# A Mamba-2 layer inside a trunk kernel: TensorE's steps placed by hand, diagonal parts by pairs

## The chip, the cores and the metric

The kernel runs on one core of one Trainium2 chip. A core has TensorE (PE, matrix products into PSUM), VectorE (DVE), ScalarE (ACT, activations from tables), GpSimd (POOL) and SyncE (SP, which here issues all DMAs). Each engine works through its own instructions in order and waits at semaphores for the others. The metric is the device time of one execution in microseconds (us); lower is better.

## The reference

Two layers of a decoder trunk on 512 tokens of 1024 features. Each has a token mixer, a squared-ReLU MLP, two layer norms and a gated embedding. The change touches only the mixer of the first layer, Mamba-2 SSD: 32 heads of 64 columns in 4 groups, 4 chunks of 128 tokens. Cut to that mixer:

```python
zxbcdt = u @ w_in
z, xbc, dt = jnp.split(zxbcdt, [SSD_D_INNER, SSD_D_INNER + SSD_CONV_DIM], axis=-1)
xbc = jax.nn.silu(causal_depthwise_conv(xbc, conv_w, conv_b))       # 4 taps
xs, bm, cm = jnp.split(xbc, [SSD_D_INNER, SSD_D_INNER + SSD_BC_DIM], axis=-1)
dt = jax.nn.softplus(dt + dt_bias)
da = dt * -jnp.exp(a_log)
xdt = xs * dt[..., None]
a_cs = jnp.cumsum(da, axis=2)                                        # within a chunk
decay = segsum_exp(jnp.moveaxis(da, 2, -1))
cb = jnp.einsum('bclgn,bcsgn->bcgls', cm, bm)
y_diag = jnp.einsum('bcgls,bcgrls,bcsgrp->bclgrp', cb, decay, xdt)
decay_to_end = jnp.exp(a_cs[:, :, -1:] - a_cs)
states = jnp.einsum('bclgn,bclgr,bclgrp->bcgrpn', bm, decay_to_end, xdt)
chunk_decay = jnp.exp(a_cs[:, :, -1])
# scan over the chunks: h <- h * chunk_decay + states; prev is the h that a chunk starts with
y_off = jnp.einsum('bclgn,bcgrpn,bclgr->bclgrp', cm, prev, jnp.exp(a_cs))
y = y_diag + y_off + d_skip * xs
y = y * jax.nn.silu(z)
y = rms_norm(y by groups, norm_w)
return y @ w_out
```

## The kernel before

[...] I call these three matmuls of 512 columns a triple. A weight unit is 128 x 1024 numbers. `unit` (line 102) loads one by DMA into one of three `raw` buffers and `split` (line 109) makes its two parts: a cast on ScalarE (`whi`, line 113, six buffers) and a subtraction on VectorE (`wlo`, line 115, six buffers). Both are given a high priority, so that they are issued well ahead of the product.

The SSD mixer works by tiles j = 0 to 15 of 128 inner features, that is two heads each; a group is four tiles. Features lie on partitions, the 512 tokens in the free dimension. For a tile:

- `xz` (line 675) projects x and z with eight triples each. The first goes through `conv_silu` (line 628): a scaled copy on ScalarE, three taps on VectorE (line 634), silu on ScalarE (line 635). The second goes through silu alone (line 683). Before a group's first tile, `bc_group` (line 647) does the same for the group's B and C, and `bc_prep` (line 656) turns B to tokens on partitions (`btok`) and makes the masked products of C and B (`cbm`).
- `core` (line 686) loads the tile's cumulated decays from DRAM (`csb`), turns xs to tokens (line 693), multiplies it by dt (`xdt`, line 701) and by the decay to the chunk's end (`xw`, line 700). Three products with `btok` give the chunks' states (line 705); the chain from chunk to chunk is a copy, and for each of two further chunks a product and a sum (lines 712 to 715). The decay matrix `m` takes eight subtractions, an exponential and a product with `cbm` (lines 721 to 725). Eight matmuls on 64 columns each give the diagonal part (`yd`, line 735), three more the part carried from the states (`yo`, line 741). Lines 748 to 751 put y together.
- The group's output product `ssd_out` (line 775) runs once the group's root mean square is there: `rms_group` (line 762) sums the squares on TensorE (line 767, on 64 columns again) and takes the square root on ScalarE (line 771).

The loop over j (from line 783) writes these parts one after the other: projections of tile j, then `core` of tile j - 1. The order on each engine is not the written one: a planner with priorities places all instructions, those of TensorE too, by what it expects of their times. PSUM has eight banks: four for projections (`pj`), one for transposes and sums (`pt`), one for states (`pm`), two for `py0` (diagonal) and `py1` (carried). Of the work buffers, xs, z and the convolution have two each, `xdt`, `xw`, `pv`, `ecs` and `y` one. ScalarE holds one table of functions at a time; going from silu to exp or to the square root means a table load (ACT_TABLE_LOAD).

Of the kernel before, what the change touches and what calls it, by code (L numbers as in the profile page):

```python
# [15 lines left out]
P = 128  # L16
# [28 lines left out]
def trunk(ctx: ExitStack, tc, a):  # L45
# [25 lines left out]
    def f32(t):  # L71
        return t.bitcast(F32)

    two = dict(xs=2, sz=2, cv=2, cm=2, cbm=2)
    mlp = dict(r=8, blk=2, sg=2)
    bufs = dict(ssd=dict(two, ss=2), mlp0=mlp, hgrn=dict(two, xs=4, sz=4, cv=4, y=2, pv=2, btok=2, sc=2, scb=2, qd=2), mlp1=mlp)
    phase = []

    def begin(name):
# [539 lines left out]
    def dt_tail():  # L619
# [5 lines left out]
        nc.vector.tensor_copy(t, pt[:, : 3 * P].rearrange("p (i c h) -> p i c h", i=3, c=NCH))  # L625
        return t[:, 0], t[:, 2], t[:, 1]

    def conv_silu(ps, i, out):

        cv = tmp("cv", [P, T])  # L630
        nc.scalar.activation(cv, ps, AF.Identity, scale=convw[:, i, 3:4], bias=convb[:, i : i + 1])  # L631
        for k in range(3):
            d = 3 - k
            nc.vector.scalar_tensor_tensor(cv[:, d:], ps[:, : T - d], convw[:, i, k : k + 1], cv[:, d:], ALU.mult, ALU.add)  # L634
        nc.scalar.activation(out, cv, AF.Silu)
# [3 lines left out]
    def projected(i):  # L639

        if i < 4:
            return first[i]
        ps = bank(psj, "pj")
        project(unit(wssd[i - 4]), x_s, ps)
        return ps

    def bc_group(g):
        bcm = []
        for which in range(2):
            ps = projected(10 * g + which)  # L650
            t = tmp(("bm", "cm")[which], [P, T])
            conv_silu(ps, 16 + 4 * which + g, t)
            bcm.append(t)
        return bcm

    def bc_prep(bcm):
# [5 lines left out]
        nc.scalar.copy(btok, pt[:, : 3 * P].rearrange("p (c n) -> p c n", c=3))  # L662
# [8 lines left out]
        return btok, cbm, cm  # L671

    toks = []

    def xz(j):
        ps = projected(10 * (j // 4) + 2 + 2 * (j % 4))
        xs = tmp("xs", [P, T])
        conv_silu(ps, j, xs)
        if j == 1:
            toks.extend(dt_tail())  # L680
        ps = projected(10 * (j // 4) + 3 + 2 * (j % 4))
        sz = tmp("sz", [P, T])
        nc.scalar.activation(sz, ps, AF.Silu)
        return xs, sz

    def core(j, xs, sz, y, toks, btok, cbm, cm, ss=None):
        dt_tok, w_tok, cs_tok = toks
        csb = mk(w4, [P, 2, T], "a")
        nc.sync.dma_start(csb, bass.AP(tensor=csd.tensor, offset=csd.offset + 2 * j * T, ap=[[0, P], [T, 2], [1, T]]))

        pt = bank(pst, "pt")
        for c in range(NCH):
            nc.tensor.transpose(pt[:, c * P : (c + 1) * P], xs[:, c * P : (c + 1) * P], ident)  # L693
        xdt = tmp("xdt", [P, 8, 64])
        v = pt.rearrange("p (c h q) -> p (c h) q", c=NCH, h=2)
        xdt4 = xdt.rearrange("p (c h) q -> p c h q", c=NCH)
        hs = slice(2 * j, 2 * j + 2)
        ptv = pt.rearrange("p (c h q) -> p c h q", c=NCH, h=2)
        xw = tmp("xw", [P, 3, 2, 64])
        nc.vector.tensor_mul(xw, ptv[:, 0:3], bc(w_tok[:, 0:3, hs], 3, 64))  # L700
        nc.vector.tensor_mul(xdt4, ptv, bc(dt_tok[:, :, hs], 3, 64))

        pst_ = bank(psm, "pm")
        for c in range(3):
            nc.tensor.matmul(  # L705
                pst_[:, c * P : (c + 1) * P], btok[:, c, :], xw[:, c].rearrange("p h q -> p (h q)"), start=True, stop=True
            )
        cd = mk(sm, [P, 2, NCH], "cd")
        nc.scalar.activation(cd, csb.rearrange("p h (c l) -> p h c l", c=NCH)[:, :, :, P - 1], AF.Exp)
        pv = tmp("pv", [P, 3, 2, 64])  # L710
        stv = pst_[:, : 3 * P].rearrange("p (c h q) -> p c h q", c=3, h=2)
        nc.vector.tensor_copy(pv[:, 0], stv[:, 0])
        for c in range(1, 3):
            nc.vector.tensor_mul(pv[:, c], pv[:, c - 1], bc(cd[:, :, c], 2, 64))
            nc.vector.tensor_add(pv[:, c], stv[:, c], pv[:, c])

        m = mk(w4, [P, 2, T], "b")
        for r in range(2):
            for c in range(NCH):
                sl = slice(c * P, (c + 1) * P)  # L720
                nc.vector.tensor_scalar(
                    m[:, r, sl], csb[:, r, sl], cs_tok[:, c, 2 * j + r : 2 * j + r + 1], 0.0, ALU.subtract, ALU.min
                )
        nc.scalar.activation(m, m, AF.Exp)
        nc.vector.tensor_mul(m, m, bc(cbm, 1, 2))

        ecs = tmp("ecs", [P, 3 * P])
        for r in range(2):
            rs = slice(64 * r, 64 * r + 64)
            nc.scalar.activation(ecs[rs], csb[rs, r, P:], AF.Exp)  # L730
        yd = bank(psy, "py0")
        for c in range(NCH):
            sl = slice(c * P, (c + 1) * P)
            for r in range(2):
                nc.tensor.matmul(  # L735
                    yd[64 * r : 64 * r + 64, sl], xdt[:, 2 * c + r, :], m[:, r, sl], start=True, stop=True
                )
        ri = None if ss is None else rms_group(ss)
        yo = bank(psy, "py1")
        for c in range(1, NCH):  # L740
            nc.tensor.matmul(  # L741
                yo[:, c * P : (c + 1) * P],
                pv[:, c - 1].rearrange("p h q -> p (h q)"),
                cm[:, c * P : (c + 1) * P],
                start=True,
                stop=True,
            )
        nc.vector.scalar_tensor_tensor(y, xs, dskip[:, j : j + 1], yd, ALU.mult, ALU.add)
        nc.vector.tensor_mul(ecs, yo[:, P:], ecs)
        nc.vector.tensor_add(y[:, P:], y[:, P:], ecs)  # L750
        nc.vector.tensor_mul(y, y, sz)
        return ri

    def sq_sum(y, ss):
        sq = tmp("ss" if ss is None else "sq", [P, T])
# [16 lines left out]
        nc.vector.reciprocal(ri, ri)  # L772
        return ri

    def ssd_out(g, s, ri, *after):
        out_project(a["wso"][4 * g : 4 * g + 4], s, False, *after, scale=ri)

    pend = None
    ys = None
    bcm = None  # L780
    prep = None
    outs = []
    for j in range(17):
        nbcm = bc_group(j // 4) if j % 4 == 0 and j < 16 else None
        cur = xz(j) if j < 16 else None
        if j == 4:
            nc.sync.dma_start(acc, a["x"])
            for c in range(NCH):
                nc.vector.tensor_scalar(acc[:, c, :], acc[:, c, :], ALPHA, None, ALU.mult)
        if pend is not None:  # L790
            i = j - 1
            if i % 4 == 0:
                ys = Split(4)
                ss = None
                prep = bc_prep(bcm)
            y = tmp("y", [P, T])
            due = bool(outs) and (i % 4 == 1 or i == 15) and i != 13
            ri = core(i, *pend, y, toks, *prep, outs[0][2] if due else None)
            w = snw[:, i : i + 1]
            nc.scalar.activation(ys.h(i % 4), y, AF.Copy, scale=w)  # L800
            nc.vector.scalar_tensor_tensor(ys.l(i % 4), y, w, f32(ys.h(i % 4)), ALU.mult, ALU.subtract)
            ss = sq_sum(y, ss)
            if i % 4 == 3:
                outs.append((i // 4, ys, ss))
            if due:
                ssd_out(*outs.pop(0)[:2], ri)
        if nbcm is not None:
            bcm = nbcm
        pend = cur
# [460 lines left out]
```

## Time and profile before

| | us |
|---|---|
| median of three runs | 1425.13 |
| lowest, highest | 1424.92, 1426.70 |
| the profiled execution, device time | 1426.6 |
| its span, first to last instruction | 1424.8 |
| PE busy in the span | 1413.6 (99%) |
| DVE busy | 1057.4 (74%) |
| ACT busy | 754.5 (53%) |

The page lists how long each engine is busy; in the views by time, a row has start, duration, engine, line, operation, and which tile is written from which. In brackets stands how long the engine was idle before it and who released it. The granted clock of TensorE is 1.00 throughout. In the views by groups, `x32 | 9.1, 284 | 0.1` means 32 instructions, 9.1 us busy, 284 ns each on the mean, and 0.1 us of idle time just before them. A float32 matmul of 128 columns stands in the profile as two instructions, a transpose as one.

### The profile page before, as it was taken

The numbers are of one execution on the slowest core, as the hardware profiler recorded it, in microseconds if no ns is written. First come the engines' busy times: TensorE is split into PE (matmuls) and PEld (weight loads), VectorE is DVE, ScalarE is ACT, GpSimd is POOL, SyncE is SP. The second block draws the span as 40 slices with busy tenths as digits, with TensorE's granted clock in tenths as the row PEclk, the third lists the DMA queues.
The fourth block names the chain that finished last, engine by engine and source line by source line (L and its number), as shares of the span: only waits on it lengthen the run. The fifth ranks groups of instructions, "written<-read, shape, count | busy, mean of one in ns | idle before, by whom it ended". The sixth has DMA issues, their size and how long they took to land.

```text
span 1424.8 us, 20421 instructions
## 1 busy us (share of the span) xinstructions
PE 1413.6 (99%) x8061; PEld 1174.6 (82%) x8061; DVE 1057.4 (74%) x1760; ACT 754.5 (53%) x1134; POOL 1.8 (0%) x12
## 2 busy tenths in 40 slices
PE   9999999999999999999999999999999999999998
PEld 7888888888888888888888887887898888888887
DVE  7988687787967667677986576678685867667873
ACT  6776454563265454545545547655555454544641
POOL 0000000000000000000000000000000000000000
PEclk9999999999999999999999999999999999999999
DMA  8432323333433444444621321222163444444231
GB/s 298 142 130 92 119 89 119 104 107 126 152 119 121 158 130 153 133 148 163 215 82 49 133 90 60 75 90 90 50 232 104 148 137 145 148 133 163 89 118 45
DMA packets 49392, 178.02 MB, mean 125 GB/s; under 512 B 5521, under 2 KB 6289, under 8 KB 49169
## 3 DMA queue, kind: packets, MB, share of 16 engines
q1 hardware_dynamic: 49296, 176.73, 36.8%
q8 instruction: 63, 1.03, 0.3%
q14 instruction: 33, 0.26, 0.1%
HBM read 174.54 MB, written 2.16 MB: 124 GB/s over the span
## 4 chain that ended last, share of the span: by engine, by line
PE 94%; DVE 3%; ACT 2%; DMA 1%; issue 0%; SPq 0%; ACTq 0%; DVEq 0%
PE pj L119 23%; PE pj L120 23%; PE pj L121 23%; PE py L119 5%; PE py L121 5%; PE py L120 5%; PE py L735 1%; PE py L741 1%; PE py L981 1%; PE pm L705 1%; DVE wlo L115 1%; PE pt L233 1%; PE pt L693 1%; DMA r<-in_w 1%; PE py L1107 0%
## 5 line engine op out<-in xcount | busy, mean ns | idle before, releaser
L113 ACT CAST whi<-raw 128x1024 fp32r<-128x1024 f32 x222 | 233.0, 1052 | 330.3 <-PE pj L120 234.1
L119 PE MATMUL pj<-b,whi 128*128 128x512 f32 (+1 forms) x1006 | 382.1, 381 | 0.7 <-ACT b L237 0.7
L120 PE MATMUL pj<-b,whi 128*128 128x512 f32 (+1 forms) x1006 | 380.6, 379 | 1.0 <-DVE b L238 1.0
L121 PE MATMUL pj<-b,wlo 128*128 128x512 f32 (+1 forms) x1006 | 379.2, 377 | 0.0
L115 DVE TENSOR_TENSOR wlo<-raw,whi 128x1024 fp32r<-128x1024 f32 x222 | 269.8, 1220 | 142.2 <-ACT whi L113 136.8
L120 PEld LDWEIGHTS pj<-b,whi 128*128 128x128 f32 x1006 | 189.4, 188 | 34.2 <-DVE b L238 1.2
L119 PEld LDWEIGHTS pj<-b,whi 128*128 128x128 f32 x1006 | 188.9, 188 | 34.1 <-ACT b L237 0.9
L121 PEld LDWEIGHTS pj<-b,wlo 128*128 128x128 f32 x1006 | 189.2, 188 | 33.6
L121 PE MATMUL pj<-whi,b 128*128 128x512 f32 x544 | 212.8, 392 | 0.0
L119 PE MATMUL pj<-whi,b 128*128 128x512 f32 x536 | 212.7, 397 | 0.0
L120 PE MATMUL pj<-wlo,b 128*128 128x512 f32 x536 | 210.2, 393 | 0.0
L121 PEld LDWEIGHTS pj<-whi,b 128*128 128x128 f32 x544 | 102.1, 188 | 20.9
L119 PEld LDWEIGHTS pj<-whi,b 128*128 128x128 f32 x536 | 100.7, 188 | 20.6 <-ACT b L1128 0.6
L120 PEld LDWEIGHTS pj<-wlo,b 128*128 128x128 f32 x536 | 100.8, 188 | 19.4
L113 ACT CAST whi<-r 128x1024 fp32r<-128x1024 f32 x72 | 75.7, 1053 | 67.8 <-PE pj L121 38.6
L115 DVE TENSOR_TENSOR wlo<-r,whi 128x1024 fp32r<-128x1024 f32 x72 | 87.6, 1219 | 23.8 <-ACT whi L113 23.2
L121 PE MATMUL py<-whi,b 128*128 128x512 f32 (+1 forms) x250 | 96.9, 388 | 0.0
L120 PE MATMUL py<-wlo,b 128*128 128x512 f32 x224 | 87.2, 389 | 0.0
L119 PE MATMUL py<-whi,b 128*128 128x512 f32 x224 | 87.1, 390 | 0.0
L121 PEld LDWEIGHTS py<-whi,b 128*128 128x128 f32 x250 | 46.9, 188 | 9.7
L634 DVE SCALAR_TENSOR_TENSOR cv<-pj,cst,cv 128x509 f32<-128x509 f32 (+2 forms) x66 | 48.7, 744 | 3.6 <-ACT cv L631 2.8
L119 PEld LDWEIGHTS py<-whi,b 128*128 128x128 f32 x224 | 42.1, 188 | 9.1 <-DVE sg L494 0.3
(303 smaller groups left out, 1864.7 us busy)
## 6 DMA issues: line engine op xcount, KB each, us to landing
raw<-in_w SPq DMA_DIRECT2D x112, 512.0 KB, 3.3
r<-in_w SPq DMA_DIRECT2D x64, 512.0 KB, 3.4
raw<-in_wssd SPq DMA_DIRECT2D x36, 512.0 KB, 3.4
a<-csd SPq DMA_DIRECT2D x16, 512.0 KB, 3.6
raw<-in_wso SPq DMA_DIRECT2D x16, 512.0 KB, 3.3
raw<-in_wg SPq DMA_DIRECT2D x16, 512.0 KB, 3.4
raw<-in_whq SPq DMA_DIRECT2D x16, 512.0 KB, 3.3
raw<-in_whvg SPq DMA_DIRECT2D x14, 512.0 KB, 3.2
```

Of the source, the lines that this page charges most:

```text
L113: nc.scalar.copy(hi[:, :n], f)
L115: nc.vector.tensor_sub(lo[:, :n], f, f32(hi[:, :n]))
L119: nc.tensor.matmul(out, sh, mh, start=start, stop=False, **kw)
L120: nc.tensor.matmul(out, sh, ml, start=False, stop=False, **kw)
L121: nc.tensor.matmul(out, sl, mh, start=False, stop=stop, **kw)
L233: nc.tensor.transpose(pt[:, j * P : (j + 1) * P], src[:, k * P : (k + 1) * P], ident)
L634: nc.vector.scalar_tensor_tensor(cv[:, d:], ps[:, : T - d], convw[:, i, k : k + 1], cv[:, d:], ALU.mult, ALU.add)
L693: nc.tensor.transpose(pt[:, c * P : (c + 1) * P], xs[:, c * P : (c + 1) * P], ident)
L705: nc.tensor.matmul(pst_[:, c * P : (c + 1) * P], btok[:, c, :], xw[:, c].rearrange("p h q -> p (h q)"), start=True, stop=True)
L735: nc.tensor.matmul(yd[64 * r : 64 * r + 64, sl], xdt[:, 2 * c + r, :], m[:, r, sl], start=True, stop=True)
L741: nc.tensor.matmul(yo[:, c * P : (c + 1) * P], pv[:, c - 1].rearrange("p h q -> p (h q)"), cm[:, c * P : (c + 1) * P], start=True, stop=True,)
L981: nc.tensor.matmul(pcs[r][bs, at : at + n], kk[r][:, ts], qs, start=True, stop=True)
```

## The change

The parts of `core` become functions of their own (`enter`, `states`, `carried`, `diagonal`), and the projections become generators that stop after each triple. `period` runs the projections of two tiles, triple by triple, and calls the parts at triples given by number, inside `tc.manual_schedule`, which keeps TensorE's instructions in the order in which they are written. The other engines are still placed by the planner.

The diagonal parts of two tiles come right behind each other, one in `py0` and one in `py1`, seven times; tiles 14 and 15 stand alone. The chain of the states uses one operation that multiplies and adds, for each head of 64 columns, in place of a product and a sum over both heads; these steps and the sums of squares get a higher priority. The output products of groups 0 to 2 are cut in halves (`partial`) and put between the projections of later periods; those of group 2 run in the last period. The buffers of xs and z go from two to four, those of `xdt`, `ecs` and `y` from one to two.

```diff
-    bufs = dict(ssd=dict(two, ss=2), ...
+    bufs = dict(ssd=dict(two, xs=4, sz=4, xdt=2, ecs=2, y=2, ss=2), ...
     def projected(i):
         if i < 4:
             return first[i]
         ps = bank(psj, "pj")
-        project(unit(wssd[i - 4]), x_s, ps)
+        hi, lo = unit(wssd[i - 4])
+        for k in range(8):
+            c = slice(k * P, (k + 1) * P)
+            mm3(ps, hi[:, c], lo[:, c], x_s.h(k), x_s.l(k), k == 0, k == 7)
+            if k < 7:
+                yield
         return ps
...
+    def states(j):
...
-        nc.vector.tensor_copy(pv[:, 0], stv[:, 0])
-        for c in range(1, 3):
-            nc.vector.tensor_mul(pv[:, c], pv[:, c - 1], bc(cd[:, :, c], 2, 64))
-            nc.vector.tensor_add(pv[:, c], stv[:, c], pv[:, c])
+        with tc.high_priority(offset=SOON):
+            nc.vector.tensor_copy(pv[:, 0], stv[:, 0])
+            for c in range(1, 3):
+                for r in range(2):
+                    nc.vector.scalar_tensor_tensor(pv[:, c, r], pv[:, c - 1, r], cd[:, r, c : c + 1], stv[:, c, r], ALU.mult, ALU.add)
...
+    def diagonal(js, rms=None):
+        yds = []
+        for n, j in enumerate(js):
+            yd = bank(psy, "py%d" % n)
+            for c in range(NCH):
+                ...
+                    nc.tensor.matmul(
+                        yd[64 * r : 64 * r + 64, sl], tiles[j]["xdt"][:, 2 * c + r, :], tiles[j]["m"][:, r, sl], start=True, stop=True
+                    )
+            yds.append(yd)
+        if rms is not None:
+            groups[rms]["ri"] = rms_group(groups[rms]["ss"])
+        for j, yd in zip(js, yds):
...
+    def partial(g, h):
+        units = [unit(a["wso"][4 * g + 2 * h + i]) for i in range(2)]
...
+    def period(p, work, at):
+        n = 0
+        for item in work:
+            for _ in item:
+                n += 1
+                for f in at.pop(n, ()):
+                    f()
...
-    for j in range(17):
-        nbcm = bc_group(j // 4) if j % 4 == 0 and j < 16 else None
-        cur = xz(j) if j < 16 else None
-        ...
+    with tc.manual_schedule(engines={mybir.EngineType.PE}):
+        period(0, [bc_group(0), xz(0), xz(1)], {})
+        toks.extend(dt_tail())
+        plan = at((8, bc_prep), (10, enter, 0), (16, states, 0), (20, enter, 1), (25, carried, 0), (26, states, 1))
+        period(1, [xz(2), xz(3)], plan)
+        plan = at((1, carried, 1), (2, enter, 2), (8, diagonal, (0, 1)), (10, states, 2), (14, enter, 3), (20, carried, 2), (21, states, 3))
+        plan |= at((28, carried, 3), (33, diagonal, (2, 3)), (35, bc_prep), (37, enter, 4), (44, states, 4))
+        period(2, [bc_group(1), xz(4), xz(5)], plan)
+        for p in range(3, 8):
+            i, b = 2 * p - 1, p // 2
+            if p % 2:
+                work = [xz(i + 1), xz(i + 2)]
+                work.insert(0 if p == 7 else 2, partial(*((1, 1) if p == 7 else (b - 1, 0))))
+                plan = at((2, carried, i - 1), (5, enter, i), (12, states, i), (19, carried, i), (25, diagonal, (i - 1, i), b - 1))
+                if p < 7:
+                    plan |= at((17, enter, i + 1), (27, states, i + 1), (36, carried, i + 1))
+                else:
+                    plan |= at((31, enter, 14), (37, states, 14), (44, carried, 14))
+            else:
+                work = [bc_group(b), xz(i + 1), xz(i + 2)]
+                if p == 4:
+                    work.insert(1, partial(0, 1))
+                n = 16 * len(work) - 48
+                plan = at((5, enter, i), (12, states, i), (20, carried, i), (26, diagonal, (i - 1, i)))
+                plan |= at((33 + n // 2, bc_prep), (37 + n, enter, i + 1), (44 + n, states, i + 1))
+            period(p, work, plan)
+        plan = at((1, diagonal, (14,)), (4, enter, 15), (10, states, 15), (16, carried, 15), (20, diagonal, (15,)))
+        period(8, [partial(2, 0), partial(2, 1)], plan)
     h_s, *after = norm(0)
-    g, s, ss = outs.pop(0)
-    ssd_out(g, s, rms_group(ss), *after)
+    out_project(a["wso"][12:16], groups[3]["ys"], False, *after, scale=rms_group(groups[3]["ss"]))
```

More of the change, by code (lines that the diff above doesn't have):

```diff
@@ L72, in f32 @@
         return t.bitcast(F32)
-    two = dict(xs=2, sz=2, cv=2, cm=2, cbm=2)
+    two = dict(cv=2, cm=2, cbm=2)
     mlp = dict(r=8, blk=2, sg=2)
-    bufs = dict(ssd=dict(two, ss=2), mlp0=mlp, hgrn=dict(two, xs=4, sz=4, cv=4, y=2, pv=2, btok=2, sc=2, scb=2, qd=2), mlp1=mlp)
+    bufs = dict(ssd=dict(two, xs=4, sz=4, xdt=2, ecs=2, y=2, ss=2), mlp0=mlp, hgrn=dict(two, xs=4, sz=4, cv=4, y=2, pv=2, btok=2, sc=2, scb=2, qd=2), mlp1=mlp)
     phase = []
@@ L626, in dt_tail @@
         return t[:, 0], t[:, 2], t[:, 1]
+    toks = []
     def conv_silu(ps, i, out):
@@ L643, in projected, with bc_prep @@
         ps = bank(psj, "pj")
-        project(unit(wssd[i - 4]), x_s, ps)
+        hi, lo = unit(wssd[i - 4])
[4 more added lines that the diff above has]
+                yield
         return ps
+    bcm = []
     def bc_group(g):
-        bcm = []
+        new = []
         for which in range(2):
-            ps = projected(10 * g + which)
+            ps = yield from projected(10 * g + which)
             t = tmp(("bm", "cm")[which], [P, T])
             conv_silu(ps, 16 + 4 * which + g, t)
-            bcm.append(t)
-        return bcm
-    def bc_prep(bcm):
+            new.append(t)
+            if g:
+                yield
+        bcm[:] = new
+    prep = []
+    def bc_prep():
         bm, cm = bcm
@@ L670, in bc_prep @@
         )
-        return btok, cbm, cm
-    toks = []
+        prep[:] = btok, cbm, cm
+    tiles = {}
     def xz(j):
[L676 to L689, printed above, removed]
+        d = tiles[j] = dict()
+        ps = yield from projected(10 * (j // 4) + 2 + 2 * (j % 4))
+        d["xs"] = tmp("xs", [P, T])
+        conv_silu(ps, j, d["xs"])
+        if j:
+            yield
+        ps = yield from projected(10 * (j // 4) + 3 + 2 * (j % 4))
+        d["sz"] = tmp("sz", [P, T])
+        nc.scalar.activation(d["sz"], ps, AF.Silu)
+        if j:
+            yield
+        if j == 4:
+            nc.sync.dma_start(acc, a["x"])
+            for c in range(NCH):
+                nc.vector.tensor_scalar(acc[:, c, :], acc[:, c, :], ALPHA, None, ALU.mult)
@@ L691, in core, with enter @@
+    def enter(j):
+        d = tiles[j]
+        d["csb"] = mk(w4, [P, 2, T], "a")
+        nc.sync.dma_start(d["csb"], bass.AP(tensor=csd.tensor, offset=csd.offset + 2 * j * T, ap=[[0, P], [T, 2], [1, T]]))
         pt = bank(pst, "pt")
         for c in range(NCH):
[L693 to L696, printed above, removed]
+            nc.tensor.transpose(pt[:, c * P : (c + 1) * P], d["xs"][:, c * P : (c + 1) * P], ident)
+        dt_tok, w_tok, _ = toks
+        d["xdt"] = tmp("xdt", [P, 8, 64])
@@ L703, in core @@
+    def states(j):
+        d = tiles[j]
+        csb, cs_tok = d["csb"], toks[2]
+        btok, cbm, cm = prep
         pst_ = bank(psm, "pm")
@@ L705, in core @@
             nc.tensor.matmul(
-                pst_[:, c * P : (c + 1) * P], btok[:, c, :], xw[:, c].rearrange("p h q -> p (h q)"), start=True, stop=True
+                pst_[:, c * P : (c + 1) * P], btok[:, c, :], d["xw"][:, c].rearrange("p h q -> p (h q)"), start=True, stop=True
             )
@@ L725, in core, with carried @@
         nc.vector.tensor_mul(m, m, bc(cbm, 1, 2))
-        ecs = tmp("ecs", [P, 3 * P])
+        d["ecs"] = tmp("ecs", [P, 3 * P])
         for r in range(2):
             rs = slice(64 * r, 64 * r + 64)
[L730 to L738, printed above, removed]
+            nc.scalar.activation(d["ecs"][rs], csb[rs, r, P:], AF.Exp)
+    def carried(j):
+        d = tiles[j]
+        cm = prep[2]
         yo = bank(psy, "py1")
@@ L742, in core @@
                 yo[:, c * P : (c + 1) * P],
[L743 removed]
+                d["pv"][:, c - 1].rearrange("p h q -> p (h q)"),
                 cm[:, c * P : (c + 1) * P],
@@ L747, in core @@
             )
[L748 to L752, printed above, removed]
+        nc.vector.tensor_mul(d["ecs"], yo[:, P:], d["ecs"])
+    groups = {}
+    def diagonal(js, rms=None):
+        yds = []
+        for n, j in enumerate(js):
+            yd = bank(psy, "py%d" % n)
+            for c in range(NCH):
+                sl = slice(c * P, (c + 1) * P)
+                for r in range(2):
+                    nc.tensor.matmul(
[5 more added lines that the diff above has]
+        for j, yd in zip(js, yds):
+            d = tiles.pop(j)
+            if j % 4 == 0:
+                groups[j // 4] = dict(ys=Split(4), ss=None)
+            g = groups[j // 4]
+            ys = g["ys"]
+            y = tmp("y", [P, T])
+            nc.vector.scalar_tensor_tensor(y, d["xs"], dskip[:, j : j + 1], yd, ALU.mult, ALU.add)
+            nc.vector.tensor_add(y[:, P:], y[:, P:], d["ecs"])
+            nc.vector.tensor_mul(y, y, d["sz"])
+            w = snw[:, j : j + 1]
+            nc.scalar.activation(ys.h(j % 4), y, AF.Copy, scale=w)
+            nc.vector.scalar_tensor_tensor(ys.l(j % 4), y, w, f32(ys.h(j % 4)), ALU.mult, ALU.subtract)
+            with tc.high_priority(offset=SOON):
+                g["ss"] = sq_sum(y, g["ss"])
+    def partial(g, h):
+        units = [unit(a["wso"][4 * g + 2 * h + i]) for i in range(2)]
+        for c in range(NCH):
+            sl = slice(c * P, (c + 1) * P)
+            ps = bank(psj, "pj")
+            for k in range(4):
+                hi, lo = units[k // 2]
+                ks = slice((k % 2) * 512, (k % 2 + 1) * 512)
+                mm3(ps, groups[g]["ys"].h(k, sl), groups[g]["ys"].l(k, sl), hi[:, ks], lo[:, ks], k == 0, k == 3)
+                if k < 3:
+                    yield
+            d = acc[:, c, h * 512 : (h + 1) * 512]
+            nc.vector.scalar_tensor_tensor(d, ps, groups[g]["ri"][:, c : c + 1], d, ALU.mult, ALU.add)
+            yield
     def sq_sum(y, ss):
@@ L773, in rms_group @@
         return ri
[L775 to L782, printed above, removed]
-    for j in range(17):
-        nbcm = bc_group(j // 4) if j % 4 == 0 and j < 16 else None
-        cur = xz(j) if j < 16 else None
[L786 to L809, printed above, removed]
@@ new lines, in period, with at @@
+    def period(p, work, at):
[5 more added lines that the diff above has]
+                    f()
+        assert not at, (p, n, at.keys())
+    def at(*places):
+        plan = {}
+        for n, f, *args in places:
+            plan.setdefault(n, []).append(lambda f=f, args=args: f(*args))
+        return plan
+    with tc.manual_schedule(engines={mybir.EngineType.PE}):
[26 more added lines that the diff above has]
+        period(8, [partial(2, 0), partial(2, 1)], plan)
```

10 lines of the change are left out of this document (5 added, 5 removed).

## The prediction

> **What bounds the kernel now.** I read the page's span first, then the busy times of the stage that the change touches, from about 44 us (the first transposes of a tile) to about 350 us (the last group's root mean square), then the matmuls of that stage in order of time.
>
> ```profile
> span 1424.8 us, 20421 instructions
> ```
> ```profile
> 44.00:350.00 306.00, 305.79 (x1709) 252.96 (x1708) 247.95 (x481) 179.14 (x235) 0.00 (x0) 1.00 0.33 109
> ```
> The columns of the second row are the stretch, its length, and the busy time of TensorE (PE), its weight loads, VectorE (DVE), ScalarE (ACT) and GpSimd, then the granted clock, 1.00. TensorE is busy for 305.79 of 306.00 us. A busy TensorE still hides small losses, since its matmuls overlap in the record, so I read them by their starts.
>
> ```profile
> 252.02 0.60 PE L693 MATMUL pt<-cst,xs 128*128 128x128 f32 x4
> 252.37 0.48 PE L119 MATMUL pj<-b,whi 128*128 128x512 f32 x1
> 252.69 0.40 PE L120 MATMUL pj<-b,whi 128*128 128x512 f32 x1
> 252.92 0.40 PE L121 MATMUL pj<-b,wlo 128*128 128x512 f32 x1
> 253.15 0.39 PE L119 MATMUL pj<-b,whi 128*128 128x512 f32 x1
> 253.38 0.83 PE L705 MATMUL pm<-xw,btok 128*128 128x128 f32 x6
> 254.14 1.09 PE L735 MATMUL py<-b,xdt 128*64 128x128 f32 x16
> 255.16 0.49 PE L741 MATMUL py<-cm,pv 128*128 128x128 f32 x2
> 255.41 0.47 PE L120 MATMUL pj<-b,whi 128*128 128x512 f32 x1
> 255.72 0.39 PE L121 MATMUL pj<-b,wlo 128*128 128x512 f32 x1
> ```
> A large matmul takes 0.23 us from start to start (252.69, 252.92, 253.15, 253.38), so a triple, the unit in which the change counts its steps, takes 0.69. Four transposes and the matmul behind them take 0.67 (252.02 to 252.69), 0.11 for each small one and 0.23 for the large: breaking into a projection costs next to nothing. The diagonal part, on 64 columns, does cost something:
>
> ```profile
> 128.62 1.09 PE L735 MATMUL py<-b,xdt 128*64 128x128 f32 x16
> 129.55 0.63 PE L767 MATMUL pt<-ones_s,ss 128*64 128x64 f32 x16
> ```
> Here 16 of its matmuls are followed by others on 64 columns, and take 0.93, 0.058 each. Above, from 253.38 to 255.72, stand 8 small matmuls (0.88), 16 on 64 columns (0.93) and one large (0.23): 2.04 of 2.34 us. So 0.30 goes into entering and leaving the 64-column form, up to 0.35 if the overlap within the 16 is better than 0.058. The other loss I find is one wait:
>
> ```profile
> 44.04 0.39 PE L119 MATMUL pj<-b,whi 128*128 128x512 f32 x1
> 44.64 0.66 PE L693 MATMUL pt<-cst,xs 128*128 128x128 f32 x4 [0.21 <-ACT btok L662]
> ```
> From 44.04 to 44.64 is 0.60, so 0.37 is lost. The stage therefore holds little to win: its matmuls are all kept, and a gain can come only from these two.
>
> **The change part by part.** *Diagonal parts by pairs.* Before, there is one 64-column stretch for each of 16 tiles; the built order shows the last tile's in two pieces and the last rms group by itself: 18. After, there are seven pairs (three take the rms group along), two single tiles and the last rms group: 10. Eight entries and exits less, at 0.30 to 0.35: 2.6 us gained (2.4 to 2.8). The wait at 44 us goes too, as tile 0's transposes now come ten triples into the second period: 0.4. Together 3.0.
>
> *The states' chain.*
>
> ```profile
> L714 DVE TENSOR_TENSOR pv<-pv,cd 128x128 f32<-128x128 f32 x32 | 9.1, 284 | 0.1
> ...
> L1093 DVE SCALAR_TENSOR_TENSOR pv<-pv,y,pm 128x128 f32<-128x128 f32 x8 | 2.8, 344 | 3.4 <-ACT pv L1091 3.3
> ```
> Four operations of 128 columns (0.284) become four of 64 columns that multiply and add at once. None of these is in the trace; the same operation on 128 columns takes 0.344, so one takes between half of that and all of it, and I take 0.28. For 64 of them that is 0 us of VectorE time (-7 to +4), in a stage where VectorE idles for 58 us (247.95 of 306.00). The chain is not what TensorE waits for: its reader (carried) stands seven triples, 4.8 us, behind the states' matmuls. I price it at 0; its cover is those seven triples.
>
> *TensorE's order by hand.* Before, the planner placed the small matmuls; now they stand at fixed triples, and TensorE stops where an operand is late. Whether it is follows from the order of the other queues, each served in order.
>
> ```profile
> ACT whi L113 <- PE pj L120: 241.4, 86, 5.5
> ```
> ScalarE's cast of a weight unit waits for TensorE to release one of six buffers, 86 times and up to 5.5 us. Whatever ScalarE has queued behind that cast waits as well. Its prices and VectorE's, from two stretches in order of time:
>
> ```profile
> 125.26 1.05 ACT L113 CAST whi<-raw 128x1024 fp32r<-128x1024 f32 x1
> 126.32 1.28 ACT L683 ACT_TABLE_LOAD   x1
> 127.62 0.60 ACT L683 ACTIVATE sz<-pj 128x512 f32<-128x512 f32 x1
> 128.11 0.62 ACT L635 ACTIVATE xs<-cv 128x512 f32<-128x512 f32 x1
> 128.75 1.28 ACT L771 ACT_TABLE_LOAD   x1
> 130.23 0.26 ACT L771 ACTIVATE ri<-pt,cst 128x4 f32<-128x4 f32 x1 [0.20 <-PE pt L767]
> ```
> ```profile
> 53.66 0.55 DVE L750 TENSOR_TENSOR y<-y,ecs 128x384 f32<-128x384 f32 x1
> 54.12 0.74 DVE L634 SCALAR_TENSOR_TENSOR cv<-pj,cst,cv 128x509 f32<-128x509 f32 x1
> 54.78 0.68 DVE L751 TENSOR_TENSOR y<-y,sz 128x512 f32<-128x512 f32 x1
> 55.38 0.74 DVE L634 SCALAR_TENSOR_TENSOR cv<-pj,cst,cv 128x510 f32<-128x510 f32 x1
> 56.04 1.21 DVE L115 TENSOR_TENSOR wlo<-raw,whi 128x1024 fp32r<-128x1024 f32 x1
> 57.17 0.74 DVE L801 SCALAR_TENSOR_TENSOR b<-y,cst,b 128x512 fp32r<-128x512 f32 x1
> 57.84 0.74 DVE L634 SCALAR_TENSOR_TENSOR cv<-pj,cst,cv 128x511 f32<-128x511 f32 x1
> 58.50 0.54 DVE L700 TENSOR_TENSOR xw<-pt,toks 128x384 f32<-128x384 f32 x1
> 58.96 0.68 DVE L701 TENSOR_TENSOR xdt<-pt,toks 128x512 f32<-128x512 f32 x1
> 59.56 1.21 DVE L115 TENSOR_TENSOR wlo<-raw,whi 128x1024 fp32r<-128x1024 f32 x1
> ...
> 63.90 0.86 DVE L721 TENSOR_SCALAR b<-a,toks 128x128 f32<-128x128 f32 x4
> ```
> From start to start VectorE takes 0.66 for a tap or another 512-column multiply-add, 0.60 for a 512-column product, 0.46 for a 384-column one, 1.13 for the cast's remainder, 0.19 for one of the 128-column subtractions. An engine starts 0.05 after the other ends (129.55 + 0.63 = 130.18, then 130.23). I went through the built order with these, placing each step of TensorE by 0.69 a triple, and find six places where it must wait.
>
> 1. enter(6), period 3, triple 17. ScalarE's queue holds, ahead of xs(6), the cast of the unit for group 2's cm. Its buffer is the one of z(6), read last in triple 16. From there: 0.05, cast 1.05, table load 1.30, silu 0.62, 0.05: 3.1. TensorE has one large matmul and one triple left, less the 0.16 by which a matmul (0.39) outlasts the next one's start: 0.76. A wait of 2.3 (2.0 to 2.6).
> 2. enter(14), period 7, triple 31. xs(14) stands behind the square of y(12), which VectorE makes after the diagonal pair of triple 25. From the cast that waits for triple 24: 1.10; then on VectorE its remainder 1.13, three taps and y's multiply-add 2.64, add 0.55, reciprocal 0.1, product 0.68; on ScalarE the square 0.62, table load 1.30, silu 0.62, and 0.15 between engines: 8.9. TensorE has 0.76, the pair 32 x 0.058 + 0.30, the rms group 0.6, six triples 4.14: 7.6. A wait of 1.3 (0.9 to 1.6).
> 3. states(3), period 2, triple 21. From the states(2) matmuls on, VectorE has queued, ahead of xw(3), the copy and four short steps (5 x 0.20), two taps and three multiply-adds (3.3), two adds (0.92), two products and a sum (1.8), eight subtractions (1.55), and xw 0.54: 9.2 with the hand-over. TensorE has eleven triples (7.6), 4 + 6 small ones (1.1), less 0.16, and 0.1 of switching: 8.5. A wait of 0.7 (0.3 to 1.1).
> 4. diagonal(2,3), the same backlog one product later: 0.3 (0 to 0.7).
> 5. and 6. The rms groups of periods 3 and 5 need the bank that xdt still reads; xdt stands behind a cast that waits for triple 24: 0.05, 1.05, remainder 1.18, xdt 0.68, 0.05: 3.0, against 0.76 and the pair's 1.85: 0.4 each (0.2 to 0.6).
>
> Sum 2.3 + 1.3 + 0.7 + 0.3 + 0.8 = 5.4; for some 60 other placed steps I add 0.2 of waits too short to list (0 to 1). So 5.6 lost, 3.0 gained: +2.6 us. What is hidden: each tile's decay load goes out with enter, seven triples (4.8 us) ahead of its reader, and lands in 3.6.
>
> ```profile
> a<-csd SPq DMA_DIRECT2D x16, 512.0 KB, 3.6
> ```
> On the SP queue it stands between weight loads and may hold them while its buffer is read; the six buffers of cast weights cover that. The built order has 17 table loads more in the stage, 17 x 1.28 = 22 us on an engine that idles for 127; they cost only where places 1 and 2 count them. The projection of the output is cut in halves and spread; its matmuls stay. After the stage all queues are in the same order as before.
>
> [...]
>
> **The sum.** The profiled execution took 1426.6 us, its span 1424.8 and 1.8 around it; the runs' median is 1425.13, so that run is 1.5 above it. The difference of 2.6 us is taken from the span's stretches and put on the median: 1425.13 + 2.6 = 1427.7 us.
>
> **The rivals.** *VectorE's backlog reaches further (slower).* Place 3 and 4 hang on VectorE's queue being 9.2 us long where 8.5 are there. If it is longer than my rows by 5% in the first three periods (about 40 us of work), 2.0 us more fall on states(3), the pair (2,3) and the tiles behind: 1429.7, up to 1431. It decides from about 2% on, 0.8 us. For it: the new steps stand close together there. Against it: the rows are the same operations.
>
> *The waits are not there (faster).* If casts and activations run a little earlier than the built order's prices say, place 1 alone stays, 2.3, against 3.0: 1424.4; with none, 1422.1. For it: the trace of before shows hardly a wait of TensorE in this stage. Against it: place 1 follows from a buffer that is released too late, not from a duration.
>
> [...]
>
> **How the numbers follow.** Less than 0.2% (2.9 us, 1422.3 to 1428.0) is about what a measurement of this kernel can tell from no change. My forecast, a loss of 0.5 to 4 us, has 0.60; the backlog 0.22; the faster rival 0.15; the drain 0.03. Of the forecast about six tenths lies within 0.2% (0.36) and the rest above; of the faster rival 0.07 ends below 1422.3 and 0.08 within. With a little of the backlog within: faster 0.07, same 0.46, slower 0.47. The range 1423.4 to 1431.2 reaches to place 1 alone and to the far end of the backlog; the forecast's own range is 1425.6 to 1429.1.
>
> **What would show it.** Among TensorE's waits: one of some 2 us before the transposes of period 3, released by ScalarE's xs, one of about 1 us of the same kind near 307 us, and one before the states' matmuls near 85 us, released by VectorE's xw; 64-column stretches of 32; none but short waits elsewhere. If the first of these is missing, my reading of the buffer's release is wrong, and the time falls to the faster rival.

## The result, and the profile after

The changed kernel takes 1428.34 us (median of 13 runs, 1427.64 to 1430.12), the kernel before beside it 1425.53 (13 runs, 1424.45 to 1426.70): a ratio of 1.0022, with an interval of 1.0013 to 1.0030. It is 2.8 us slower. Two further sets of the same kernel gave 1.0022 (1.0012 to 1.0031) and 1.0024 (1.0013 to 1.0034), with 3.3 and 3.5 us between the medians.

The profiled execution of it took 1428.96 us. First its span, then the stage from 44 to 350 us with the same columns as before (stretch, length, TensorE, weight loads, VectorE, ScalarE, GpSimd, granted clock, then the DMA engines' busy share and GB/s).

```profile
span 1427.2 us, 20422 instructions
```
```profile
44.00:350.00 306.00, 301.49 (x1682) 250.29 (x1682) 242.38 (x479) 198.27 (x250) 0.00 (x0) 0.99 0.33 109
```

TensorE, busy for 305.79 of these 306.00 us before, now lacks 4.51, and its mean clock is 0.99 in place of 1.00. Its waits name the places (us in all, times, the longest):

```profile
PE pt L712 <- ACT xs L637: 3.5, 2, 2.3
...
PE pm L727 <- DVE xw L718: 0.5, 1, 0.5
PE pt L830 <- DVE xdt L719: 0.5, 2, 0.3
```

These are the transposes of tiles 6 and 14, the states of tile 3, and the two root mean squares of periods 3 and 5. TensorE in order of time around the longest:

```profile
124.94 0.39 PE L121 MATMUL pj<-b,wlo 128*128 128x512 f32 x1
127.64 0.66 PE L712 MATMUL pt<-cst,xs 128*128 128x128 f32 x4 [2.31 <-ACT xs L637]
...
128.83 0.51 PE L119 MATMUL pj<-b,whi 128*128 128x512 f32 x1
129.13 0.63 PE L120 MATMUL pj<-b,whi 128*128 128x512 f32 x1
129.56 0.63 PE L121 MATMUL pj<-b,wlo 128*128 128x512 f32 x1
129.99 1.48 PE L760 MATMUL py<-cm,pv 128*128 128x128 f32 x6
131.12 0.77 PE L119 MATMUL pj<-b,whi 128*128 128x512 f32 x1
```

Two things stand here. From 124.94 to 127.64 is 2.70, of which 0.23 is the large matmul: 2.47 lost. And from 129.13 on the large matmuls start 0.43 apart (129.13, 129.56, 129.99) in place of 0.23. The same stretch by slices of one microsecond (the clock is the third column from the end):

```profile
128.00:129.00 1.00, 1.00 (x7) 0.87 (x6) 0.56 (x1) 0.98 (x2) 0.00 (x0) 0.98 1.06 184
129.00:130.00 1.00, 1.00 (x4) 0.70 (x4) 0.00 (x0) 0.58 (x2) 0.00 (x0) 0.50 0.66 266
130.00:131.00 1.00, 1.00 (x6) 1.00 (x5) 0.00 (x0) 0.00 (x0) 0.00 (x0) 0.50 0.37 148
131.00:132.00 1.00, 1.00 (x5) 0.90 (x4) 0.49 (x1) 0.00 (x0) 0.00 (x0) 0.50 0.00 0
132.00:133.00 1.00, 1.00 (x5) 0.78 (x5) 0.07 (x1) 0.00 (x0) 0.00 (x0) 0.82 0.06 16
```

The lost clock adds up to 0.02 + 0.50 x 3 + 0.18 = 1.70 us, that is 3.4 us at half. A busy TensorE at half its clock shows as busy, so the waits don't tell of this; the start-to-start times do, and give 1.6 us. I had not predicted it.

The second wait, at tile 14:

```profile
311.52 0.39 PE L121 MATMUL pj<-b,wlo 128*128 128x512 f32 x1
313.10 0.66 PE L712 MATMUL pt<-cst,xs 128*128 128x128 f32 x4 [1.19 <-ACT xs L637]
```

From start to start this is 1.582 unrounded, of which 0.227 is the large matmul: 1.36 lost, and here the clock stays at 1.00. By the same reckoning the states of tile 3 lose 0.69, the two root mean squares 0.93 together, the pair of tiles 2 and 3 loses 0.17.

ScalarE before the first wait shows what it waited behind:

```profile
119.90 1.05 ACT L113 CAST whi<-raw 128x1024 fp32r<-128x1024 f32 x1
124.59 1.05 ACT L113 CAST whi<-raw 128x1024 fp32r<-128x1024 f32 x1 [3.65 <-DMA raw<-in_wssd]
125.66 1.28 ACT L637 ACT_TABLE_LOAD   x1
126.95 0.63 ACT L637 ACTIVATE xs<-cv 128x512 f32<-128x512 f32 x1
```

The cast stands idle for 3.65 us at the head of the queue, then table load and silu follow as predicted. The row names the weights' transfer as what came last. The buffer's last reader, the middle matmul of triple 16 at 124.04, ended at 124.43, so that here the buffer and the transfer came within about 0.1 of each other. Which of the two comes last changes from profile to profile: in that of the kernel called again2 below the cast starts 0.44 after the same matmul ends and TensorE's wait is 2.6, in that of enter6_late the matmul itself is the releaser (3.51 idle before the cast).

### The profile page after: what moved, and what is told of

Its sections match the earlier page's. It is cut to its first block, busy times and chain, and to the rows that moved or that the text cites. A ratio compares the mean times of both kernels' runs of the same rounds, so it can differ in the third digit from the quotient of the medians.

```text
span 1427.2 us, 20422 instructions
## 1 busy us (share of the span) xinstructions
PE 1412.6 (99%) x8061; PEld 1174.4 (82%) x8061; DVE 1053.6 (74%) x1760; ACT 776.5 (54%) x1151; POOL 1.9 (0%) x12
## 4 chain that ended last, share of the span: by engine, by line
PE 94%; DVE 3%; ACT 2%; issue 0%; DMA 0%; ACTq 0%; SPq 0%; DVEq 0%
PE pj L119 24%; PE pj L120 23%; PE pj L121 23%; PE py L119 5%; PE py L120 5%; PE py L121 5%; PE pt L233 1%; PE py L1053 1%; PE py L760 1%; DVE wlo L115 1%; PE pm L727 1%; PE py L779 1%; PE pt L712 0%; PE py L1179 0%; ACT whi L113 0%
```

## The experiments

Tile numbers, triples and names are those of the code above; a triple is the three matmuls of `mm3`: high by high, high by low and low by high part. To compare executions without the scatter of the rest of the kernel I also use the length of the stage in each profile, from the start of the 101st matmul of 256 or 512 columns (28 to 29 us) to that of the 1401st, counted from the back so that the extra ones of a kernel do not shift it (376 to 384 us): 350.62 before, 355.02 after.

The stage is 4.40 longer, the whole profiled span only 2.4 (1427.2 after 1424.8). The other 2.0 lie outside the stage and scatter between executions. Ahead of it, the 101st matmul starts at 29.27 before and at 28.50 after; the recorded clock first becomes full at 7.62 and at 6.08. Behind it, one wait near 1047 us took 1.2 before and 0.2 after.

**The changed kernel again.** No edit. Two theories of the dip are set against each other from here on. Theory A: the wait lets the clock drop, in a part of the executions. Theory B: the dip has nothing to do with the wait, so the share of executions with it is the same in every kernel of a set.

> The changed kernel once more, as the level for the three others on the same chip: 1428.3 us. In the profile of it the granted clock is 0.50 for some 3.4 us right behind the wait at 125 us. [...]

Measured: 1429.06 us (1428.63 to 1429.85) against 1425.77 before. 8 of 10 executions show a mean clock below 1.000, and 10 of 32 of the kernel before beside it, which speaks against theory B. The 8 take 1429.3 us on the mean, the other two 1428.7. The level of the changed kernel on this chip is 0.7 above the first set's.

**Tile 6's transposes later.**

```diff
-plan |= at((17, enter, i + 1), (27, states, i + 1), (36, carried, i + 1))
+plan |= at((22 if p == 3 else 17, enter, i + 1), (27, states, i + 1), (36, carried, i + 1))
```

> Tile 6's transposes stand at triple 22 of period 3 in place of 17; nothing else is moved. Theory A: the wait of 2.47 us (start to start) goes, and with it the dip of the clock (1.6 us in about half of the executions): 1428.3 - 2.5 - 0.9 = 1424.9, mean clock 1.000 throughout, although the wait of 1.36 us near 309 us stays. Theory B: only the wait goes, 1425.8, and half of the executions still show a clock below 1.000. Rival C (VectorE's or ScalarE's backlog is the real limit, so the wait turns up again a few triples later): not below 1427.3.

Measured: 1425.58 us (1425.02 to 1426.95), 3.5 less than the changed kernel beside it; ratio to before 1.0000 (0.9991 to 1.0009). Stage 350.76. The remaining wait of this kind is tile 14's:

```profile
PE pt L712 <- ACT xs L637: 1.2, 1, 1.2
```

One number moved by five triples takes the whole net loss back: 2.5 us of wait and about 1.0 more. Nothing turns up further on, so rival C falls. On the clock, 4 of 11 executions are still below 1.000, but so are 21 of 84 of the kernel before, whose profile shows no dip in the stage. The traces show another drop that can account for these: in the profiles of the kernel before and of the changed one the clock is at half in the last microseconds of the span, when TensorE has made its last matmul (before: from 1424.15 of 1424.8 on, after the last matmul's end at 1420.89; after: from 1426.02 of 1427.2 on, after 1423.25). So the clock of the kernel before is not 1.00 to the very end, but that drop has no matmul left to slow.

**Tile 14's transposes later.**

```diff
-plan |= at((31, enter, 14), (37, states, 14), (44, carried, 14))
+plan |= at((34, enter, 14), (40, states, 14), (47, carried, 14))
```

> Tile 14's transposes, states and carried parts stand at triples 34, 40 and 47 of period 7 in place of 31, 37 and 44. The wait of 1.36 us (start to start) goes: 1427.0; the dip of the clock behind the wait at 125 us stays in about half of the executions. Rival C: the wait moves to the transposes or to the single diagonal part behind them, and the time stays at 1428.3.

Measured: 1427.32 us (1426.52 to 1428.46), 1.7 less than the changed kernel beside it, against 1.4 expected. The wait at tile 14 is gone and none takes its place:

```profile
PE pt L712 <- ACT xs L637: 2.4, 1, 2.4
```

In this profile the 2.4 us of wait at tile 6 are there and the clock does not drop behind them (1.00 from 122 to 140 us; stage 351.97, which is 355.02 - 1.36 - 1.6 to within 0.1). So a drop stands behind this wait in one execution and not in another; what differs between them was not shown.

**Tile 6's transposes one triple later.**

```diff
-plan |= at((17, enter, i + 1), (27, states, i + 1), (36, carried, i + 1))
+plan |= at((18 if p == 3 else 17, enter, i + 1), (27, states, i + 1), (36, carried, i + 1))
```

> As the changed kernel, but tile 6's transposes stand one triple later, at 18 of period 3: the wait there should be 2.5 - 0.7 = 1.8 us (start to start). [...] If any wait of more than 1.5 us drops the clock: 1428.3 with the clock of the changed kernel.

Measured: 1427.46 us (1426.46 to 1429.08) beside 1425.68 before.

```profile
PE pt L712 <- ACT xs L637: 2.8, 2, 1.6
```

The wait became shorter by just the triple (start to start 1.78 after 2.47): moving the step did not move what it waits for. 10 of 11 executions have a clock of 1.000, the profiled one among them. So this wait of 1.6 us has no drop of the clock behind it in the profile, and the 1428.3 with the clock of the changed kernel did not come.

**The wait filled with work.**

```diff
 pt = bank(pst, "pt")
+for _ in range(10 if j == 6 else 0):
+    nc.tensor.matmul(pt, x_s.h(0)[:, :P], x_s.h(0), start=True, stop=True)
 for c in range(NCH):
```

> As the changed kernel, but in front of tile 6's transposes TensorE makes ten large products (10 x 0.227 = 2.27 us) into the bank that the transposes overwrite, so that the stretch is busy and as long as the wait was. The products are extra work that no result uses. Theory A: the delay stays, the idle time goes and so does the dip of the clock: 1428.3 - 0.9 = 1427.4, mean clock 1.000 in all executions. Theory B: 1428.3, with a clock below 1.000 in half of them.

Measured: 1428.96 us (1427.63 to 1430.48) against 1429.06 beside it. The clock is as theory A has it: no dip in the profile, 8 of 11 executions at 1.000 and three at 0.999. The slices of this kernel's profile:

```profile
128.00:129.00 1.00, 1.00 (x6) 0.78 (x5) 0.55 (x1) 1.00 (x1) 0.00 (x0) 1.00 0.79 160
129.00:130.00 1.00, 1.00 (x9) 0.96 (x8) 0.00 (x0) 0.25 (x2) 0.00 (x0) 1.00 0.76 287
130.00:131.00 1.00, 1.00 (x6) 0.81 (x5) 0.56 (x1) 0.00 (x0) 0.00 (x0) 1.00 0.34 131
```

The stage is 353.25, so 1.8 shorter, with the same delay at tile 6. The time of the whole is not: behind the stage this profile waits longest at another place.

```profile
PE pj L120 <- DVE b L238: 1.6, 1, 1.6
```

This wait, near 1047 us, hangs on a transfer of weights in a later stage; start to start it took 1.2 in the profile before, 0.2 in the one after, 0.5 in the second one and 1.8 here. It scatters by itself, and one profile can't say whether it gives back what the stage gained. Hence a second set.

> The changed kernel as the level for the filled one beside it: 1428.3 to 1429.1 us, a mean clock of 0.9991 over the executions (as in the 34 executions so far of kernels with the wait of 2.5 us).

> The ten large products in place of the wait once more (extra work that no result uses), because the first set showed the clock without the dip (0.9997 on the mean) but the time unchanged (1428.96 against 1429.06), within the scatter of some 0.4. Theory A (the dip is on the path): 0.8 less than the changed kernel beside it. Rival F (what the dip takes is given back further on, at a wait near 1047 us that the weights' transfers set, so it costs nothing in the end): no difference, within 0.3, at a clock of 0.9997.

Measured: 1428.91 us (8 runs) and 1428.89 (6 runs); in the second profile of the filled kernel the stage was again short (353.22) and the late wait 0.8. Neither profile of the filled kernel has the dip, and its time has none of the gain. Of its 17 executions 12 have a clock of 1.000 and four 0.999, much as in the kernel before; one, at 1431.05 us, has 0.998, which no execution of the kernel before has. It was not profiled, and its cause stays open. That the time does not fall speaks for rival F, but the other comparisons don't: enter6_late gained 1.0 more than its shorter wait explains, the kernel with tile 6 one triple later 0.3 to 1.0 more (by the three sets' 2.8 to 3.5, as no changed kernel ran beside it), though enter14_late, which keeps that wait, also gained 0.4 more; and among the 31 executions of the changed kernel the 20 with a clock below 1.000 took 1429.2 us on the mean, the 11 at 1.000 took 1428.2, while in the kernel before (21 and 63 executions) there is no such difference (1425.6 and 1425.7). What the dip costs in the end stays open between 0 and 1.0 us.

**All late steps moved.**

```diff
-(8, diagonal, (0, 1)), (10, states, 2), (14, enter, 3), (20, carried, 2), (21, states, 3)
-(28, carried, 3), (33, diagonal, (2, 3)), (35, bc_prep), (37, enter, 4), (44, states, 4)
+(8, diagonal, (0, 1)), (10, states, 2), (14, enter, 3), (21, carried, 2), (23, states, 3)
+(30, carried, 3), (36, diagonal, (2, 3)), (38, bc_prep), (40, enter, 4), (46, states, 4)
-(25, diagonal, (i - 1, i), b - 1), (17, enter, i + 1), (27, states, i + 1), (36, carried, i + 1)
+(26, diagonal, (i - 1, i), b - 1), (28, enter, i + 1), (35, states, i + 1), (42, carried, i + 1)
-(31, enter, 14), (37, states, 14), (44, carried, 14)
+(34, enter, 14), (40, states, 14), (47, carried, 14)
```

> The pairs are kept, and every step of TensorE that waits in the changed kernel is moved back by a few triples: in period 2 carried(2) 21, states(3) 23, carried(3) 30, the pair (2,3) 36, the preparation 38, enter(4) 40, states(4) 46; in periods 3 and 5 enter(i+1) 28, states 35, carried 42; in period 7 enter(14) 34, states 40, carried 47; the pairs of the odd periods at 26 in place of 25. Theory A: gone are 2.5 (period 3) + 1.4 (period 7) + 0.7 (states of tile 3) + 0.5 (two groups' root mean squares) + 0.2 (pair of tiles 2 and 3) and the dip of the clock, 0.8 on the mean: 6.1 less than the changed kernel's 1429.0, so 1422.9, and 2.9 less than the kernel before. Rival C (the planner's queues are the limit, the waits come back behind the moved steps): 1425 or more.

Measured: 1422.29 us (1421.68 to 1423.69); ratio to before 0.9978 (0.9970 to 0.9987), 3.4 us faster than before and faster than both kernels. TensorE's stage:

```profile
44.00:350.00 306.00, 306.00 (x1728) 255.29 (x1727) 246.27 (x481) 198.55 (x251) 0.00 (x0) 1.00 0.33 110
```

306.00 of 306.00. Rival C falls here too: the queues of ScalarE and VectorE, with the same work in nearly the same order, keep up once TensorE asks a few triples later.

**The pairs undone in it.**

```diff
 for n, f, *args in places:
+    if f is diagonal and len(args[0]) == 2:
+        plan.setdefault(n - 2, []).append(lambda j=args[0][0]: product(j, 0))
```

(product makes the 8 products of one tile, which are 16 matmuls in the profile; diagonal then makes only the second tile's.)

> As all_moved, but the pairs are undone: the first tile's diagonal products stand two triples ahead of the second's, so there are seven 64-column stretches more. By the prediction's price of 0.30 to 0.35 us for entering and leaving the form: 2.1 to 2.5 us more than all_moved. Rival D (the pairs were never worth anything, the stretches before were only crowded): the same as all_moved within 0.5.

Measured: 1424.73 us (1423.57 to 1426.55), 2.44 above all_moved: 0.35 for each of seven stretches. By the stage it is 350.15 after 347.51, or 0.38 each. Rival D falls. One such stretch:

```profile
97.08 0.39 PE L121 MATMUL pj<-b,wlo 128*128 128x512 f32 x1
97.40 1.09 PE L776 MATMUL py<-b,xdt 128*64 128x128 f32 x16
98.42 0.50 PE L119 MATMUL pj<-b,whi 128*128 128x512 f32 x1
98.76 0.40 PE L120 MATMUL pj<-b,whi 128*128 128x512 f32 x1
99.00 0.39 PE L121 MATMUL pj<-b,wlo 128*128 128x512 f32 x1
```

and the same place in all_moved, with 32:

```profile
97.45 0.39 PE L121 MATMUL pj<-b,wlo 128*128 128x512 f32 x1
97.77 1.97 PE L779 MATMUL py<-b,xdt 128*64 128x128 f32 x32
99.66 0.50 PE L119 MATMUL pj<-b,whi 128*128 128x512 f32 x1
100.00 0.40 PE L120 MATMUL pj<-b,whi 128*128 128x512 f32 x1
100.24 0.39 PE L121 MATMUL pj<-b,wlo 128*128 128x512 f32 x1
```

From first to last row 1.92 and 2.79: the 16 more take 0.87, or 0.054 each, and 1.92 - 3 x 0.227 - 0.87 = 0.37 is left in either for going in and out.

**The old chain in it.**

```diff
-for r in range(2):
-    nc.vector.scalar_tensor_tensor(pv[:, c, r], pv[:, c - 1, r], cd[:, r, c : c + 1], stv[:, c, r], ALU.mult, ALU.add)
+nc.vector.tensor_mul(pv[:, c], pv[:, c - 1], bc(cd[:, :, c], 2, 64))
+nc.vector.tensor_add(pv[:, c], stv[:, c], pv[:, c])
```

> As all_moved, but with the states' chain as it was before: a product and a sum of 128 columns for each of two steps in place of four multiply-adds of 64 columns. By the prediction, which prices the chain at nothing because VectorE idles and seven triples cover it: the time of all_moved within 0.4. Rival E (four dependent steps hold the carried parts up): 0.5 us or more above all_moved, with a wait of TensorE on pv or on a bank whose reader stands behind the chain.

Measured: 1423.38 us (1421.96 to 1424.03), 1.09 above all_moved by the medians and 0.70 by the means, the latter only just clear of the executions' scatter (0.65 by a 95% interval); the stage is 349.03 after 347.51. The profile has one wait that all_moved lacks, in the carried parts of one tile:

```profile
125.36 0.60 PE L760 MATMUL py<-cm,pv 128*128 128x128 f32 x4
127.19 0.49 PE L760 MATMUL py<-cm,pv 128*128 128x128 f32 x2 [1.23 <-DVE pv L738]
```

VectorE in that stretch:

```profile
122.45 0.28 DVE L735 COPY pv<-pm 128x128 f32<-128x128 f32 x1
122.65 0.28 DVE L744 TENSOR_SCALAR b<-a,toks 128x128 f32<-128x128 f32 x1
122.84 0.29 DVE L737 TENSOR_TENSOR pv<-pv,cd 128x128 f32<-128x128 f32 x1
123.04 1.23 DVE L115 TENSOR_TENSOR wlo<-raw,whi 128x1024 fp32r<-128x1024 f32 x1
124.17 0.29 DVE L738 TENSOR_TENSOR pv<-pm,pv 128x128 f32<-128x128 f32 x1
124.37 1.22 DVE L115 TENSOR_TENSOR wlo<-raw,whi 128x1024 fp32r<-128x1024 f32 x1
125.50 0.30 DVE L737 TENSOR_TENSOR pv<-pv,cd 128x128 f32<-128x128 f32 x1
125.71 1.23 DVE L115 TENSOR_TENSOR wlo<-raw,whi 128x1024 fp32r<-128x1024 f32 x1
126.84 0.29 DVE L738 TENSOR_TENSOR pv<-pm,pv 128x128 f32<-128x128 f32 x1
```

and in all_moved, where the four short steps stand side by side:

```profile
120.63 0.29 DVE L735 COPY pv<-pm 128x128 f32<-128x128 f32 x1
120.84 0.28 DVE L744 TENSOR_SCALAR b<-a,toks 128x128 f32<-128x128 f32 x1
121.03 0.85 DVE L738 SCALAR_TENSOR_TENSOR pv<-pv,cd,pm 128x64 f32<-128x64 f32 x4
```

Between dependent steps the planner places other work, here a weight's remainder of 1.2 us each time. The chain lasts 4.7 us from copy to last sum in place of 1.3. Part of the delay is that the copy itself came late (122.45 after 120.63): ScalarE's exponent of the decays waited there for its load and started at 119.16, in all_moved at 117.92. The two weren't told apart.

**The new chain in the kernel before.** The reverse edit in the kernel before, nothing else.

> The kernel before with the new chain alone: four multiply-adds of 64 columns in two dependent steps in place of the product and the sum of 128 columns in four; TensorE's order is left to the planner. By the prediction: 1425.6 within 0.4. Rival E (the chain's latency counts by itself): 0.5 us or more below the kernel before. As the planner orders VectorE's queue anew around the shorter chain, the wait of 0.4 at 44 us may move; that is inside the 0.4.

Measured: 1424.94 us (1423.67 to 1426.09), ratio 0.9996 (0.9987 to 1.0005): by that interval not to be told from no change. By the medians it is 0.50 below the kernel before beside it, which is just rival E's bound, and by the means 0.65. So this run does not decide between the two.

## Why the prediction was right

The forecast was +2.6 us to 1427.7; the measured +2.8 to 1428.34 lies in the forecast's own range. By its steps:

- *Places 1 to 6.* Predicted 2.3, 1.3, 0.7, 0.3 and 0.4 + 0.4; start to start they lose 2.47, 1.36, 0.69, 0.17 and 0.93: 5.6 against 5.4. At place 3 the prediction's own terms for TensorE add up to 8.6 and not 8.5, which would have given a wait of 0.6; measured were 0.69. The two that were put down to ScalarE's queue each went when its own step alone was moved. Of place 1's cause only half was named: the cast waits for the buffer and for the transfer of its weights, which come within 0 to 0.4 us of each other.
- *64-column stretches.* Predicted 0.30 to 0.35 each and 2.6 for eight; seven measured 2.44 in the median and 2.64 in the stage, so 0.35 to 0.38 each.
- *The wait at 44 us.* None in the profile after; but in the profile of the second repetition the transposes of tile 0 waited 0.9 for btok near 48 us, and in that of the kernel before with the new chain 0.9 stand at 44 us. It varies between executions by more than the 0.4 that I booked.
- *Table loads.* ScalarE's instructions rose from 1134 to 1151 and its busy time from 754.5 to 776.5 us: 17 and 22, as the built order gave it, hidden but for places 1 and 2.
- *The chain.* One step takes 0.275 us (predicted 0.28). "I price it at 0; its cover is those seven triples" is the step in doubt, though the sum does not show it: in the kernel before the new chain measured 0.5 to 0.65 less, at the edge of what the executions tell from nothing, and in all_moved the old chain costs 0.7 to 1.1, with a wait on it in the profile. In the changed kernel itself the old chain was not tried. I had counted the chain as its four steps, and not what the planner puts between steps that depend on each other.
- *What was missing.* The half clock behind place 1. The clocks of all executions say how often: kernels with the wait of 2.5 us have a mean clock of 0.9991 (42 executions), the kernel before 0.99975 (84): 0.0006 x 1427 = 0.9 us of lost clock on the average. With it the difference would be 2.6 to 3.5, which holds the three sets (2.8, 3.3, 3.5). The prediction put this at nothing, and that the first set came within 0.2 of the forecast is luck in part. In the profiles the stage without the dip is 4.40 - 1.6 = 2.8 longer, against the 2.6 forecast; this, and the places one by one, is what bears the mechanism out.
- *The rivals.* The waits are all there, so the faster one fell. VectorE's backlog ended at place 4, with 0.17 us there. A drain at the table switches, given a chance of 0.03, shows in no run: a load takes 1.28 us and the next activation mostly follows at once (125.66 + 1.28 = 126.94, and the silu starts at 126.95; at 61 of the profile's 69 loads the next activation starts within 0.1 us).

## What to carry to other kernels

Where an order by hand replaces a planner's, go through the other queues at each placed step: a step that comes three triples too early costs its wait (1.36 us at tile 14), and moving that one number gives it back. A row of 64-column matmuls cost some 0.35 us once here, for 32 of them as for 16 (2.44 us for seven rows more), so gather them. A chain of short dependent steps can become as long as what the planner places between them (4.7 us in place of 1.3 in one profile here), so count its dependences before its elements.

## What the runs showed of the hardware

Around a wait of TensorE of 2.3 to 2.6 us its clock is halved in a part of the executions. The profiles of the changed kernel and its two repetitions show the dip, 3.41 us long in the first (128.96 to 132.37) and 3.4 to 3.5 by the slices of the others; that of enter14_late, with a wait of 2.4, doesn't show it. The dip does not follow the wait by a fixed time: it begins 1.3 and 1.2 us after the transposes start again, and in again2 0.5 us before they do. At half the clock the large matmuls start 0.43 us apart in place of 0.23.

The waits of 1.19 us at tile 14 and of 1.62 one triple later have no dip behind them in their profiles. With the wait filled by matmuls neither of two profiles shows the dip. The clocks of the executions agree: 15 of 42 executions with the wait of 2.3 to 2.6 us are at 1.000 (36%), against 63 of 84 (75%) of the kernel before. What decides in which execution the clock drops was not shown.
